# A bidirectional RWKV-7 step: the values' products move next to the first corner product, and the backward values come by DMA

## The chip, the cores and the metric

One core of a Trainium2 chip runs the whole kernel. The metric is the device time of one execution in microseconds; three executions of the kernel before took 2247.28, 2251.11 and 2251.58 us, so the median is 2251.11 us.

The core has five engines that work side by side, each through its own instruction queue in order: TensorE (PE, matmuls and transposes), VectorE (DVE), ScalarE (ACT), GpSimd (POOL) and SyncE (SP), which here issues nearly all DMAs. An instruction waits on semaphores for what other engines and DMAs have to finish, and all that stands behind it in its queue waits too.

## The reference

One layer of a hybrid model runs on 128 context tokens and 256 latent tokens, 384 in all, with 2048 channels in 32 heads of 64. One large input projection feeds an RWKV-7 branch (A) and a gated short convolution (B); both are projected, merged and projected again.

The part that matters is the scan of branch A. It runs once per direction `d`, with time reversed for `d = 1`:

```python
def step(S, inp):
    r_t, w_t, k_t, v_t, a_t, b_t = inp
    sa = jnp.einsum('dbhij,dbhj->dbhi', S, a_t)
    S = S * w_t[..., None, :] + sa[..., :, None] * b_t[..., None, :] + v_t[..., :, None] * k_t[..., None, :]
    y = jnp.einsum('dbhij,dbhj->dbhi', S, r_t)
    return S, y
```

`sa` is what a step removes from the state: it depends on the state, and so on all earlier values `v`. The values are the same in both directions, only their order in time differs.

## The kernel before, in words

**The stream.** All large products (input projection, output projections) are one long stream of matmuls on TensorE. Weights come as fp32 in halves of 1 MB (`wload`, L96, two `raw` buffers), are split by ACT and DVE into a high and a low fp32r part (`split`, L85, casts on L88, subtractions on L89, three buffers `whi` and `wlo`), and are used by three matmuls (L81 to L83). Three such matmuls are one unit, `ds_.go(n)` emits `n` units, and a quarter of a weight pair (one `whi` buffer) serves eight units, 24 matmuls.

**The blocks.** Sixteen blocks `b` of 128 channels (two heads) go through the scan, one after the other. A block's work is a set of generators: `prep_a` and `prep_k` (decays, keys), `prep_b` (chunk products and the inversion), `prep_c` (operands of the scan), `scan`, `norm`, `finish`. A generator says with `yield n` that `n` units of the stream stand between its pieces, and `drive` (L936) emits them. So the stream fills the time in which the scan waits for other engines.

**Chunks.** A direction has 384 tokens in 6 chunks of 64 tokens, so a block has 12 chunks, index `f` (0 to 5 forward, 6 to 11 backward). Within a chunk the steps become a triangular system. `A[:, 0, f, :]` holds its matrices: partitions 0 to 63 the part between removals, which must be inverted, and partitions 64 to 127 (`C:P`) the part that takes values to removals. `sav[:, f, :]` is the matching right side: partitions 64 to 127 hold the values with time on the partitions, partitions 0 to 63 the removals.

**The inversion.** Each triangular matrix is cut in 32 x 32 corners. `prep_b` writes them by DMA to DRAM (`ui`, L715) and reads them back as `U` with one corner per partition (L721). DVE eliminates column by column in 30 pairs of steps (L726, L728), and DMAs bring the inverses back into `A` (L739) and into `x11` (L740). `corner` in `scan` completes the inverse by two products of corners, `pH` and `pX` (L853).

**`prep_c` before the change.** It loads the initial states, then turns the values of both directions: three 128 x 128 transposes on TensorE (L760) of `v`, then three of `vr`, which ACT copies in reversed order from `v` (L757), and four ACT copies out of PSUM into `sav[C:P]` (L762). It turns `bk` (L769), computes the values' part of the removals by 24 products of 64 x 64 (`pav`, L775; each shows as two records) and copies them with four ACT copies into `sav[0:C]` (L779). POOL then clears `A[C:P, 0]` (L782), so that later products with all of `A[:, 0]` add no value twice.

**`scan` before the change.** It starts with `pH`, whose four copies into `x11` go to ACT and DVE in turn (L859). Then the latent chain is started (`chain(1)`: `po` L815, added to `sav` by DVE on L816), the bonus and `pX` follow, and both chains run: `pq` (L832) multiplies `A[:, 0, f]` with `sav[:, f]`, `pu` (L839) updates the states.

**What sets the order.** TensorE's order is written out by hand (`manual_schedule`, L73). The other queues, SP's among them, are ordered by a planner from dependencies, priorities and its own estimates; `scan` has a higher priority. `tc.issue_after(x)` keeps instructions behind `x` on its engine. Before `scan`, L972 to L974 fill the units since `prep_c` up to `WINDOW` = 80 (96 in the first and last block). PSUM tiles of the scans rotate through five banks (`bank`, L595).

Of the kernel before, what the change touches and what calls it, by code (L numbers as in the profile page):

```python
# [9 lines left out]
F32 = mybir.dt.float32  # L10
# [5 lines left out]
P = 128  # L16
D = 2048
KC = 16
T = 384
TC_ = 128  # L20
NB = 16
C = 64
NCH = 6
# [33 lines left out]
def hybrid_step(ctx, tc, cst, x_prompt, x_sample, state_f, state_b, c, c_ctx, ada_w, ada_b, norm_g,  # L57
                w_in, mu_prev, mu_next, w0, w2, a0, a2, k_k, k_a, r_k, lnx_g, lnx_b, conv_w,
                w_out_a, w_out_b, w_o, final_g, y_prompt, y_sample, ns_f, ns_b):
    nc = tc.nc  # L60
    V, S, G, TE = nc.vector, nc.scalar, nc.gpsimd, nc.tensor
# [8 lines left out]
    dp = ctx.enter_context(tc.tile_pool(name="dp", bufs=1, space=bass.MemoryType.DRAM))  # L70
# [5 lines left out]
    ident = cs[:, C_ID:C_ID + P]  # L76
# [176 lines left out]
    def pcol(i, n=1):  # L253
        return par[:, i:i + n]
# [151 lines left out]
    r_, k_, v_, ga_ = {}, {}, {}, {}  # L406
    box = {}

    def tmp(nm):
        return box["sp"].tile([P, T], F32, tag="t", name=nm, bufs=8)  # L410
# [141 lines left out]
    for i in range(3):  # L552
        t = tmp(f"lst_{i}")
# [4 lines left out]
    for m in range(4):  # L558
# [6 lines left out]
        t = tmp(f"lin_{m}")  # L565
# [3 lines left out]
        src = t[0:96, ::-1] if m % 2 else t[0:96, :]  # L569
# [23 lines left out]
    hss = [slice(0, C), slice(C, P)]  # L593

    def bank(nm):  # L595
        return ps1.tile([P, 4, P], F32, tag="A", name=nm, bufs=5)
# [4 lines left out]
    def flat(a):  # L601
        return a.rearrange("p n t -> p (n t)")
# [4 lines left out]
    def hl_parts(t, hi, nm):  # L607
        lo = sp.tile([P, T], F32R, tag="t", name=f"lo_{nm}", bufs=8)
        S.copy(hi[:], t[:])
        V.tensor_tensor(lo[:], t[:], hi[:].bitcast(F32), ALU.subtract)  # L610
        return hi, lo
# [129 lines left out]

    def prep_c(b, o):

        r, v, A = r_[b], v_[b], o["A"]
        for d in range(2):
            for h in range(2):
                nc.sync.dma_start(s_in[d][hss[h], hss[h]], ctx_st[d][0, 0, 2 * b + h])

        sav = sp.tile([P, 2 * NCH, P], F32, tag="sav", name=f"sav_{b}")
        bt = sp.tile([P, 2 * NCH, P], F32, tag="bt", name=f"bt_{b}")  # L750
        o["sav"], o["bkt"] = sav, bt
        for d in range(2):
            if d == 0:
                src = v
            else:
                src = tmp(f"vr_{b}")
                S.copy(src[:], v[:, ::-1])  # L757
            pv = bank(f"pv_{b}_{d}")
            for q in range(3):
                TE.transpose(pv[:, q, :], src[:, q * P:(q + 1) * P], ident)  # L760
            for e in range(2):
                S.copy(sav[C:P, NCH * d + e:NCH * d + NCH:2, :], pv[C * e:C * e + C, 0:3, :])  # L762
            yield 1
        for d in range(2):

            for n0, n1 in (((0, 4), (4, 5)), ((0, 3), (4, 6)))[d]:
                pb = bank(f"pb_{b}_{d}_{n0}")
                for n in range(n0, n1):
                    TE.transpose(pb[:, n - n0, :], o["bk"][d][:, n, :], ident)  # L769
                S.copy(bt[:, NCH * d + n0:NCH * d + n1, :], pb[:, 0:n1 - n0, :])  # L770
                yield 1
        pvs = [bank(f"pav_{b}_{d}") for d in range(2)]
        for f in range(2 * NCH):
            for h in range(2):
                TE.matmul(flat(pvs[f // NCH][hss[h]])[:, C * (f % NCH):C * (f % NCH) + C], A[C:P, 0, f, hss[h]],  # L775
                          sav[C:P, f, hss[h]], start=True, stop=True)
        for d in range(2):
            for h in range(2):
                S.copy(sav[0:C, NCH * d:NCH * d + NCH, hss[h]],  # L779
                       flat(pvs[d][hss[h]])[:, 0:NCH * C].rearrange("p (n i) -> p n i", i=C))  # L780

        G.memset(A[C:P, 0, :, :], 0.0)  # L782
        yield 2
        ks = o["kd"]
        V.tensor_tensor(ks[0][:], ks[0][:], ks[1][:, ::-1], ALU.add)
        V.scalar_tensor_tensor(ks[0][:], ks[0][:], pcol(RK + b), r[:], ALU.mult, ALU.mult)
        o["bsum"] = hl_parts(ks[0], sp.tile([P, T], F32R, tag="t", name=f"bsh_{b}", bufs=8), f"bs_{b}")
        yield 1
        pt = bank(f"psi_{b}")
        for d in range(2):  # L790
            TE.transpose(pt[:, d, :], s_in[d][:], ident)
        V.tensor_copy(st[1][:], pt[:, 0:2, :])
        yield 1

    def scan(b, o):
        A, x11, sav, bt = o["A"], o["x11"], o["sav"], o["bkt"]
# [51 lines left out]
        def corner(nm, lhs, rhs):  # L848
            pz = bank(f"{nm}_{b}")
            for f in range(2 * NCH):  # L850
                for h in range(2):
                    g = 32 * (2 * (f % 2) + h)
                    TE.matmul(flat(pz[g:g + 32])[:, 32 * (f // 2):32 * (f // 2) + 32], lhs(f, h), rhs(f, h),  # L853
                              start=True, stop=True)
            return [flat(pz[32 * j:32 * j + 32])[:, 0:192].rearrange("p (n t) -> p n t", t=32) for j in range(4)]

        pz = corner("pH", lambda f, h: A[0:32, 0, f, C * h + 32:C * h + C], lambda f, h: x11[0:32, 2 * f + h, :])
        for j in range(4):
            (S.copy, V.tensor_copy)[j % 2](x11[32:64, j::4, :], pz[j])  # L859
        yield H0  # L860
        lat = chain(1)
        next(lat)
# [9 lines left out]
        pz = corner("pX", lambda f, h: x11[32:64, 2 * f + h, :], lambda f, h: A[32:64, 0, f, C * h + 32:C * h + C])  # L872
# [16 lines left out]
        for q in range(3):  # L889
            for h in range(2):  # L890
                for d in range(2):
                    for e in range(2):
                        f = 2 * q + e if d == 0 else NCH + 5 - 2 * q - e
                        TE.matmul(py[hss[e], q, hss[h]], A[:, 1, f, hss[h]], sav[:, f, hss[h]],
                                  start=d == 0, stop=d == 1)
# [40 lines left out]
    def drive(gen, prio=0, at=None, fn=None):  # L936
        n = i = 0
        while True:
            if i == at:
                fn()  # L940
            i += 1
            with tc.high_priority(offset=prio):
                u = next(gen, None)
            if u is None:
                return n
            ds_.go(u)
            n += u
# [6 lines left out]
    for b in range(NB):  # L954
# [10 lines left out]
        n = drive(prep_c(b, cur))  # L965
# [140 lines left out]
    for half in range(2):  # L1106
# [8 lines left out]
        for s in range(3):  # L1115
# [10 lines left out]
            if half == 1:  # L1126
                f = rsf[:, s, :]
# [37 lines left out]
```

## Time and profile before

| | |
|---|---|
| time, median of three runs | 2251.11 us |
| time of the profiled execution | 2248.96 us |
| its span, first to last instruction | 2247.2 us |
| TensorE busy | 2187.8 us, 97% |
| VectorE busy | 1522.3 us, 68% |
| ScalarE busy | 1060.1 us, 47% |
| GpSimd busy | 115.7 us, 5% |
| granted TensorE clock | 0.996 |
| moved by DMA | 339.96 MB, mean 151 GB/s |

A row of the timeline has start, duration, engine, line, operation, out<-in and a count; in brackets stands the idle time before it and what ended it. `d_...` are matmuls of the stream. An engine with a `q` (SPq) is a queue issuing a DMA, and the duration is that of the issue, not of the transfer. A row of a group has the busy time and the mean duration in ns after the bar. A row of the DMA view has the size in KB and the median time from issue to landing in us. Matmuls overlap: the time between two starts says how long one takes, a single duration does not.

### The profile page before, as it was taken

How to read it: one execution, taken by the hardware profiler on the slowest of the kernel's cores; microseconds unless marked ns; L12 is line 12 of the kernel's file. 1: busy time of each engine (PE TensorE's matmuls, PEld its weight loads, DVE VectorE, ACT ScalarE, POOL GpSimd, SP SyncE). 2: the span in 40 equal slices, each digit the busy share in tenths (PEclk: the TensorE clock that was granted, in tenths of full speed). 3: DMA queues.
4: the chain of work that ended last, by engine and by line, in shares of the span. 5: the costliest groups of instructions: out<-in, count | busy, mean ns of one | idle time of the engine just before them, and what ended most of it. 6: DMA issues, size and time to landing. Idle time of an engine off the chain costs nothing.

```text
span 2247.2 us, 40428 instructions
## 1 busy us (share of the span) xinstructions
PE 2187.8 (97%) x16084; PEld 2072.0 (92%) x16084; DVE 1522.3 (68%) x3096; ACT 1060.1 (47%) x1864; POOL 115.7 (5%) x115
## 2 busy tenths in 40 slices
PE   5999999999999999999999999999999999999998
PEld 3688999999999999999999999999999999998988
DVE  3248567787777778777878787777777775444354
ACT  4245445454545455454545454546455543333333
POOL 2000010101010100000010101010100000000000
PEclk9999999999999999999999999999999999999999
DMA  9963544444444444353444444444445465886633
GB/s 337 346 205 116 147 129 132 111 127 116 110 126 118 115 117 130 112 133 102 124 108 130 114 111 131 111 115 136 127 119 143 137 184 154 289 293 230 220 131 113
DMA packets 429644, 339.96 MB, mean 151 GB/s; under 512 B 84800, under 2 KB 411024, under 8 KB 428560
## 3 DMA queue, kind: packets, MB, share of 16 engines
q1 hardware_dynamic: 427968, 335.62, 50.9%
q8 instruction: 127, 2.08, 0.4%
q10 hardware_dynamic: 432, 1.57, 0.2%
q14 instruction: 61, 0.50, 0.1%
q0 software_dynamic: 1056, 0.19, 0.1%
HBM read 307.37 MB, written 29.36 MB: 150 GB/s over the span
## 4 chain that ended last, share of the span: by engine, by line
PE 81%; DVE 7%; DMA 7%; ACT 3%; issue 1%; SPq 1%; POOLq 0%; POOL 0%; ACTq 0%; DVEq 0%
PE d_rk L81 4%; PE d_rk L83 4%; PE d_rk L82 4%; PE d_gv L81 4%; PE d_gv L82 4%; PE d_gv L83 4%; DMA raw_adah<-in_ada_w_dram 3%; PE pA L705 2%; PE d_oa L81 2%; PE d_oa L83 2%; PE d_oa L82 2%; PE d_bc L81 2%; PE d_bg L81 2%; DMA lraw<-in_w_dram 2%; PE d_bc L82 2%; PE d_bc L83 2%
## 5 line engine op out<-in xcount | busy, mean ns | idle before, releaser
L81 PE MATMUL d_rk<-h_hi,whi_rk 128*128 128x384 f32 x480 | 164.3, 342 | 0.6 <-ACT lst L554 0.6
L726 DVE TENSOR_TENSOR ut<-U 48x30 f32<-48x30 f32 (+14 forms) x480 | 154.5, 322 | 15.3 <-DMA U<-ui 3.0
L728 DVE TENSOR_TENSOR U<-U,ut 48x30 f32<-48x30 f32 (+14 forms) x480 | 154.3, 321 | 11.2
L81 PE MATMUL d_gv<-h_hi,whi_gv 128*128 128x384 f32 x480 | 161.4, 336 | 0.0
L83 PE MATMUL d_gv<-h_hi,wlo_gv 128*128 128x384 f32 x480 | 161.2, 336 | 0.0
L82 PE MATMUL d_gv<-h_lo,whi_gv 128*128 128x384 f32 x480 | 161.1, 336 | 0.0
L83 PE MATMUL d_rk<-h_hi,wlo_rk 128*128 128x384 f32 x480 | 160.6, 335 | 0.0
L82 PE MATMUL d_rk<-h_lo,whi_rk 128*128 128x384 f32 x480 | 160.6, 334 | 0.0
L88 ACT CAST whi_gv<-raw_gv 128x1024 fp32r<-128x1024 f32 (+1 forms) x64 | 63.9, 999 | 139.3 <-PE d_rk L82 90.9
L89 DVE TENSOR_TENSOR wlo_rk<-raw_rk,whi_rk 128x1024 fp32r<-128x1024 f32 x60 | 72.9, 1218 | 44.6 <-ACT whi_rk L88 38.9
L88 ACT CAST whi_rk<-raw_rk 128x1024 fp32r<-128x1024 f32 x60 | 63.0, 1053 | 80.0 <-PE d_bc L82 16.4
L81 PE MATMUL d_bc<-h_hi,whi_bc 128*128 128x384 f32 x256 | 92.5, 361 | 0.0
L81 PE MATMUL d_gb<-h_hi,whi_gb 128*128 128x384 f32 x256 | 92.5, 361 | 0.0
L81 PE MATMUL d_bg<-h_hi,whi_bg 128*128 128x384 f32 x256 | 92.4, 361 | 0.0
L81 PE MATMUL d_bx<-h_hi,whi_bx 128*128 128x384 f32 x256 | 92.4, 361 | 0.0
L81 PE MATMUL d_ma<-h_hi,whi_ma 128*128 128x384 f32 x256 | 92.0, 359 | 0.0
L81 PEld LDWEIGHTS d_rk<-h_hi,whi_rk 128*128 128x128 f32 x480 | 90.1, 188 | 1.8 <-ACT lst L554 0.9
L922 POOL TENSOR_TENSOR rs<-var,nhalf 128x6 f32<-128x6 f32 x16 | 21.2, 1325 | 1362.3 <-DVE var L920 1362.3
L81 PEld LDWEIGHTS d_gv<-h_hi,whi_gv 128*128 128x128 f32 x480 | 90.7, 189 | 0.2
L82 PEld LDWEIGHTS d_gv<-h_lo,whi_gv 128*128 128x128 f32 x480 | 90.7, 189 | 0.0
L83 PEld LDWEIGHTS d_gv<-h_hi,wlo_gv 128*128 128x128 f32 x480 | 90.7, 189 | 0.0
L81 PE MATMUL d_mb<-h_hi,whi_mb 128*128 128x384 f32 x256 | 90.6, 354 | 0.0
(320 smaller groups left out, 6655.4 us busy)
## 6 DMA issues: line engine op xcount, KB each, us to landing
raw_adah<-in_ada_w_dram SPq DMA_DIRECT2D x64, 512.0 KB, 8.7
raw_rk<-in_w_in_dram SPq DMA_DIRECT2D x60, 512.0 KB, 5.3
raw_gv<-in_w_in_dram SPq DMA_DIRECT2D x60, 512.0 KB, 5.0
raw_ma<-in_w_in_dram SPq DMA_DIRECT2D x16, 1024.0 KB, 5.6
raw_mb<-in_w_in_dram SPq DMA_DIRECT2D x16, 1024.0 KB, 5.5
raw_bc<-in_w_in_dram SPq DMA_DIRECT2D x16, 1024.0 KB, 5.5
raw_bx<-in_w_in_dram SPq DMA_DIRECT2D x16, 1024.0 KB, 5.3
raw_bg<-in_w_in_dram SPq DMA_DIRECT2D x16, 1024.0 KB, 5.6
```

The costliest lines, as they stand in the source:

```text
L81: TE.matmul(out, wh, xh, start=start, stop=False)
L82: TE.matmul(out, wh, xl, start=False, stop=False)
L83: TE.matmul(out, wl, xh, start=False, stop=stop)
L88: S.copy(hi[0:rows], src)
L89: V.tensor_tensor(lo[0:rows], src, hi[0:rows].bitcast(F32), ALU.subtract)
L705: TE.matmul(pas[h, n // 4 * 4][:, n % 4, :], bk[hss[h], n, :], pr[hss[h], n, :], start=True, stop=True)
L726: V.tensor_tensor(tv, U[:, 0:s, s:s + 1].broadcast_to([48, s, w]), U[:, s:s + 1, s + 1:].broadcast_to([48, s, w]), ALU.mult)
L728: V.tensor_tensor(U[:, 0:s, s + 1:], U[:, 0:s, s + 1:], tv, ALU.add)
L922: G.tensor_tensor(rs[:], var[:], nhalf[:], ALU.pow)
```

## The change

- The values are turned once. The copy to `vr`, its three transposes and its two copies out of PSUM go, and with them one `yield 1`.
- The backward values are made by three DMAs on SP, one after the other: the forward values from `sav` to a DRAM tile `vt` (tokens by channels), `vt` with reversed rows to a DRAM tile `vr`, and `vr` to the backward chunks of `sav`. Each moves 192 KB; the middle one goes in pieces of 64 channels, 256 B.
- The 24 `pav` products move from `prep_c` to the start of `scan`, right ahead of `pH`. Their four ACT copies stand behind the last ACT copy into `x11`, and the clearing of `A[C:P, 0]` follows. `prep_c` loses one `yield 2`.

```diff
     def prep_c(b, o):
 
-        r, v, A = r_[b], v_[b], o["A"]
+        r, v = r_[b], v_[b]
...
-        for d in range(2):
-            if d == 0:
-                src = v
-            else:
-                src = tmp(f"vr_{b}")
-                S.copy(src[:], v[:, ::-1])
-            pv = bank(f"pv_{b}_{d}")
-            for q in range(3):
-                TE.transpose(pv[:, q, :], src[:, q * P:(q + 1) * P], ident)
-            for e in range(2):
-                S.copy(sav[C:P, NCH * d + e:NCH * d + NCH:2, :], pv[C * e:C * e + C, 0:3, :])
-            yield 1
+        pv = bank(f"pv_{b}")
+        for q in range(3):
+            TE.transpose(pv[:, q, :], v[:, q * P:(q + 1) * P], ident)
+        for e in range(2):
+            S.copy(sav[C:P, e:NCH:2, :], pv[C * e:C * e + C, 0:3, :])
+
+        vt = dp.tile([T, P], F32, tag="vt", name=f"vt_{b}", bufs=2)
+        vr = dp.tile([T, P], F32, tag="vr", name=f"vr_{b}", bufs=2)
+        nc.sync.dma_start(vt[:].rearrange("(n s) c -> s n c", s=C), sav[C:P, 0:NCH, :])
+        nc.sync.dma_start(vr[:].rearrange("t (h c) -> h t c", h=2), vt[::-1, :].rearrange("t (h c) -> h t c", h=2))
+        nc.sync.dma_start(sav[C:P, NCH:2 * NCH, :], vr[:].rearrange("(n s) c -> s n c", s=C))
+        yield 1
...
-        pvs = [bank(f"pav_{b}_{d}") for d in range(2)]
-        for f in range(2 * NCH):
-            for h in range(2):
-                TE.matmul(flat(pvs[f // NCH][hss[h]])[:, C * (f % NCH):C * (f % NCH) + C], A[C:P, 0, f, hss[h]],
-                          sav[C:P, f, hss[h]], start=True, stop=True)
-        for d in range(2):
-            for h in range(2):
-                S.copy(sav[0:C, NCH * d:NCH * d + NCH, hss[h]],
-                       flat(pvs[d][hss[h]])[:, 0:NCH * C].rearrange("p (n i) -> p n i", i=C))
-
-        G.memset(A[C:P, 0, :, :], 0.0)
-        yield 2
...
+        pvs = [bank(f"pav_{b}_{d}") for d in range(2)]
+        for f in range(2 * NCH):
+            for h in range(2):
+                TE.matmul(flat(pvs[f // NCH][hss[h]])[:, C * (f % NCH):C * (f % NCH) + C], A[C:P, 0, f, hss[h]],
+                          sav[C:P, f, hss[h]], start=True, stop=True)
+        xs = None
         pz = corner("pH", lambda f, h: A[0:32, 0, f, C * h + 32:C * h + C], lambda f, h: x11[0:32, 2 * f + h, :])
         for j in range(4):
-            (S.copy, V.tensor_copy)[j % 2](x11[32:64, j::4, :], pz[j])
+            x = (S.copy, V.tensor_copy)[j % 2](x11[32:64, j::4, :], pz[j])
+            xs = x if j % 2 == 0 else xs
+        with tc.issue_after(xs.ins):
+            for d in range(2):
+                for h in range(2):
+                    S.copy(sav[0:C, NCH * d:NCH * d + NCH, hss[h]],
+                           flat(pvs[d][hss[h]])[:, 0:NCH * C].rearrange("p (n i) -> p n i", i=C))
+
+        G.memset(A[C:P, 0, :, :], 0.0)
         yield H0
```

## The prediction

> **What bounds the kernel now.** I read the page first: span, engines, the chain that ended last.
>
> ```profile
> span 2247.2 us, 40428 instructions
> ...
> PE 2187.8 (97%) x16084; PEld 2072.0 (92%) x16084; DVE 1522.3 (68%) x3096; ACT 1060.1 (47%) x1864; POOL 115.7 (5%) x115
> ...
> q1 hardware_dynamic: 427968, 335.62, 50.9%
> ...
> PE 81%; DVE 7%; DMA 7%; ACT 3%; issue 1%; SPq 1%; POOLq 0%; POOL 0%; ACTq 0%; DVEq 0%
> ```
>
> TensorE is busy 97% of the span and holds 81% of the chain. Next came TensorE's own waits between 200 and 1860 us, where the sixteen scans lie (releaser: total us, times, longest); its two largest rows are
>
> ```profile
> PE pu L839 <- ACT sav L834: 4.8, 11, 0.6
> PE pv L760 <- DVE A L711: 1.7, 1, 1.7
> ```
>
> In 1660 us TensorE waits for almost nothing. So what leaves its order shortens the kernel one for one, and only a new wait of TensorE can lengthen it. The other engines matter through such waits alone.
>
> **The change, part by part.** *The second turning leaves.* TensorE's timeline around it (start, duration, engine, line, count), in the block whose scan starts at 1004 us:
>
> ```profile
> 956.19 0.34 PE L83 MATMUL d_bc<-h_hi,wlo_bc 128*128 128x384 f32 x1
> 956.36 0.49 PE L760 MATMUL pv<-cs,vr 128*128 128x128 f32 x3
> 956.61 0.42 PE L81 MATMUL d_bc<-h_hi,whi_bc 128*128 128x384 f32 x1
> 956.87 0.34 PE L82 MATMUL d_bc<-h_lo,whi_bc 128*128 128x384 f32 x1
> ```
>
> and around the values' products, which move:
>
> ```profile
> 960.25 0.34 PE L83 MATMUL d_rk<-h_hi,wlo_rk 128*128 128x384 f32 x1
> 960.52 1.61 PE L775 MATMUL pav<-sav,A 64*64 64x64 f32 x48
> 962.06 0.45 PE L81 MATMUL d_rk<-h_hi,whi_rk 128*128 128x384 f32 x1
> 962.35 0.34 PE L82 MATMUL d_rk<-h_lo,whi_rk 128*128 128x384 f32 x1
> 962.52 0.34 PE L83 MATMUL d_rk<-h_hi,wlo_rk 128*128 128x384 f32 x1
> 962.70 0.33 PE L81 MATMUL d_rk<-h_hi,whi_rk 128*128 128x384 f32 x1
> ```
>
> Starts, not durations, are to be read, since matmuls overlap. Two plain steps of the stream take 0.35 us (962.35 to 962.70). With the three transposes of `vr` between, two steps take 956.87 - 956.19 = 0.68, so the turning costs 0.33 us a block, and 16 x 0.33 = **5.3 us** go. Its ACT work (one reversing copy, two copies out of PSUM) goes too, and is worth nothing: ACT is at 47% and no such wait stands above.
>
> *The burst.* The products alone cost 962.35 - 960.25 - 0.35 = 1.75 us. How much of it is entering and leaving? The first corner product, before which they are put, and the mean of one matmul in each group (after the bar: busy us, mean ns):
>
> ```profile
> 1003.81 0.34 PE L639 MATMUL pn<-lo_sq,bones_r 128*128 128x384 f32 x1
> 1004.08 0.62 PE L853 MATMUL pH<-x,A 32*32 32x32 f32 x48
> 1004.63 0.45 PE L81 MATMUL d_bx<-h_hi,whi_bx 128*128 128x384 f32 x1
> 1004.91 0.34 PE L82 MATMUL d_bx<-h_lo,whi_bx 128*128 128x384 f32 x1
> ```
> ```profile
> L775 PE MATMUL pav<-sav,A 64*64 64x64 f32 x768 | 25.8, 220 | 0.0
> L853 PE MATMUL pH<-x,A 32*32 32x32 f32 x768 | 9.9, 194 | 0.0
> ```
>
> The corner costs 1004.91 - 1003.81 - 0.35 = 0.75. From its first start to its last the `pav` group runs 1.61 - 0.22 = 1.39, the corner 0.62 - 0.19 = 0.43. What is left, 0.36 and 0.32, is a burst's fixed price, and one of the two can be saved. Upper bound 0.34 a block (passing from 64x64 to 32x32 tiles is free), lower bound 0 (it costs as much as leaving the stream and coming back). The rows show two parts of that price: the way in (0.27 to the first small matmul instead of 0.17, so 0.10) and the way back (962.06 to 962.35, 0.29 instead of 0.17, so 0.12). A change of tile size is still a way in, while one way back surely goes, with some of the emptying before it; I take 0.20, nearer to the way back. That is **3.2 us** over 16 blocks, bounds 0 and 5.4. The Trainium skill speaks against more (TensorEngine Tiling (Array Packing), Tiling Modes, Key Properties): changing the tiling mode, not just the tile, drains the TensorE. Taken strictly, the saving would be the lower bound, and the whole change worth the 5.3 us alone; no row here has two tile sizes next to each other.
>
> *Three units fewer in the preparation.* A unit is three matmuls of the stream. `prep_c` asks for 10 now and 7 then, but a block is filled up to 80 (`WINDOW`), so the three come back before the scan: moved, not saved.
>
> *What moves onto the scan's start.* The four `sav` copies, now ACT's after the second `x` copy, the POOL memset, and who needs them:
>
> ```profile
> L779 ACT COPY sav<-pav 64x384 f32<-64x384 f32 x64 | 30.4, 476 | 3.1 <-PE pav L775 2.3
> ```
> ```profile
> 1005.47 0.31 ACT L859 COPY x<-pH 32x192 f32<-32x192 f32 x1 [0.42 <-DVE x L859]
> 1007.30 1.05 ACT L88 CAST whi_bg<-raw_bg 128x1024 fp32r<-128x1024 f32 x1 [1.52 <-PE d_bx L82]
> ```
> ```profile
> 962.25 1.38 POOL L782 MEMSET A<- 64x1536 f32 x1 [8.24 <-DVE ut L726]
> ```
> ```profile
> 1011.50 0.61 PE L832 MATMUL pq<-sav,A 128*128 128x128 f32 x4
> ```
>
> The copies take 4 x 0.476 = 1.9 us: 1005.8 to 1007.7, of which 1.5 fill ACT's idle time ahead of the cast, which starts 0.4 later. DVE's sum into `sav` (L816) waits behind them with all that is queued after it on DVE, the next `wlo` first, which itself waits for that cast. The memset would end near 1005.6. TensorE asks for `sav` and `A` at 1011.5. Cover 3.8 us or more, so 0; without cover a late copy would cost TensorE its lateness once a block.
>
> *The three transfers.* No row has a DRAM-to-DRAM one. The nearest (KB, median us to landing), the copies after which the chain can start, and SP's queue there:
>
> ```profile
> uo<-U SPq DMA_DIRECT2D x16, 192.0 KB, 2.5
> U<-ui SPq DMA_DIRECT2D x16, 192.0 KB, 5.1
> ```
> ```profile
> 956.04 0.96 ACT L762 COPY sav<-pv 64x384 f32<-64x384 f32 x2 [1.01 <-PE pv L760]
> ```
> ```profile
> 956.88 0.45 SPq L721 DMA_DIRECT2D U<-ui  x1
> ...
> 968.62 1.02 SPq L104 DMA_DIRECT2D raw_gv<-in_w_in_dram  x2
> ```
>
> Each of the three waits on SP for the one before it. Lower bound 3 x 2.5 = 7.5 us. The middle one moves 768 pieces of 256 B. A packet takes 0.509 x 16 x 2247.2 us / 427968 = 43 ns on its engine on average; spread over 16 engines that is 2 us, over two engines 16 us. Upper bound 5.1 + (16.4 + 2.5) + 5.1 = 29. From 957.0 on, the values stand in `sav` by 965 to 986, and the burst wants them at 1002.3 (1004.08 - 1.75): no wait at either end. I take 9 us. What counts is SP, which issues nothing while it waits. The `U` load at 956.88 is ready as the copies end and, by this order, goes first. The next weights are issued at 968.62 and cast at 978.57:
>
> ```profile
> raw_gv<-in_w_in_dram SPq DMA_DIRECT2D x2, 512.0 KB, 4.7
> ```
> ```profile
> 978.57 1.06 ACT L88 CAST whi_gv<-raw_gv 128x1024 fp32r<-128x1024 f32 x1 [0.95 <-PE d_rk L82]
> ```
> ```profile
> 981.02 1.21 DVE L89 TENSOR_TENSOR wlo_gv<-raw_gv,whi_gv 128x1024 fp32r<-128x1024 f32 x1
> ```
>
> They land near 974, 4.5 us before the cast, which waits for TensorE to free a buffer, not for the DMA. With three buffers two quarters are then still ahead of it, 2 x 24 matmuls of 0.175 us, 8.4 us, of which cast and subtraction take 3.7 (978.57 to 982.23): another 4.7 us of cover. So these weights may come 9.2 us late, and a hold of SP of some 9 us, which is over before 968.6, costs 0. The three issues themselves are 0.4 to 1.0 us each on SP, as the rows of `U` and `x` show.
>
> *The corner's input.* TensorE now comes to `pH` 0.53 us earlier, and `x11` has to be there. Its last transfer in two blocks (issue; median us to landing in that window) and the other block's `pH`:
>
> ```profile
> 1000.19 0.91 SPq L740 DMA_DIRECT2D x<-uo  x1
> ```
> ```profile
> x<-uo SPq DMA_DIRECT2D x1, 48.0 KB, 3.5
> ```
> ```profile
> 1527.86 0.47 SPq L740 DMA_DIRECT2D x<-uo  x1
> ```
> ```profile
> x<-uo SPq DMA_DIRECT2D x1, 48.0 KB, 2.1
> ```
> ```profile
> 1532.96 0.62 PE L853 MATMUL pH<-x,A 32*32 32x32 f32 x48
> ```
>
> It lands at 1003.7, 0.4 us before `pH`; in the other block at 1530.0, 3.0 us before. These two stand for thirteen middle blocks: ten of the first kind (landing 0.3 to 1.2 ahead), three of the second (2.5 to 3.0). Blocks 0, 1 and 15 have more. If nothing else shifts, the earlier arrival waits 0.1 to 0.3 in four or five blocks, **0.5 us** in all. The cover is thin: any delay of the chain from `ui` to `x11` is paid at once in ten blocks.
>
> **Sum.** 5.3 + 3.2 - 0.5 = 8.0. The profiled execution took 2248.96 us (span 2247.2 and 1.8 around it): 2241.0. The median of the runs, 2251.11, is 2.15 higher, which gives 2243.1 on that footing. I say **2242**.
>
> **Rivals.** (a) *The wait moves to the corner: no change.* If the planner puts the first values' transfer ahead of the `U` load, that load goes out after the copies (957.0) and one issue, 0.5 us late, and has 192 KB more before it on the same DMA engines, 0.7 us at the 293 GB/s that the 16 engines reach while they are busy (335.62 MB in 50.9% of 2247.2 us). With 0.8 us of delay the ten blocks wait about 0.7 each: 8.0 - 7 = 1, 2248 to 2250. For it: both are ready within 0.2 us of each other. Against it: `U` is the older work.
>
> (b) *The chain of transfers holds what TensorE needs: slower.* Place: SP, ahead of the `U` load, with the second values' transfer there too. `U` then waits for the copies, an issue, a landing of 2.5 and another issue: 957.0 + 0.4 + 2.5 + 0.6 = 960.5, 3.6 late. Ten blocks then lose 3.5 each, three about 1: 38 us, less 8.5, is 2278. From 0.4 us of delay on, a block like the one at 1004 has lost its gain, so that the sign turns between (a) and (b). Against it: the second transfer is ready 3 us after `U` is.
>
> (c) *The middle transfer is slow: slower.* On two engines it holds SP, from 957.0, for the first transfer (0.4 + 2.5), its own issue (0.6) and 18.9, and the last issue (0.4), to 979.8. The weights of 968.62 come 11.2 us late, 2.0 more than their cover, and 13 blocks lose 26: 2267. The gain is gone once that wait is 0.6 a block, that is from a hold of about 21 us. For it, the Trainium skill (DMA: Bandwidth & Descriptors, Why a DMA increments its semaphore by 16 and not by 1) says the engines used are the largest number up to 16 that divides the slowest dimension of both patterns, and this transfer's slowest dimension is 2. Against it: pieces of 256 B are a third of the 784 B of the mean packet, and should take less than 43 ns.
>
> (d) *More than I sum:* tile sizes change for free and nothing waits: 5.3 + 5.4, 2238 to 2240.
>
> **How the numbers follow.** Forecast 0.47, (a) 0.23, (b) 0.09, (c) 0.08, (d) 0.08; 0.05 for an order of SP or DVE of which I see nothing, even either way. 0.2% (4.5 us) is about what a measurement of this kernel can tell from no change: faster is below 2246.6. The forecast's own range is 2237 to 2246.5 (sum 5 to 11, on either footing); nearly all of it, of (d) and a little of (a) is faster: 0.56. Same is most of (a) and the forecast's upper edge: 0.25. Slower is (b), (c) and the rest: 0.19. The range runs from 2235 to 2257, which leaves out (b), (c) and little below.
>
> **What would show it.** Right: 48 fewer `pv` matmuls; `pav` and `pH` side by side, from the last stream start to the second after them 2.3 + 0.35 us (2.5 without a saving, 2.16 with a full one); no wait of TensorE for a DMA at `pav` or `pH` over some tenths; `sav` copies over 3 us ahead of `pq`. Wrong: TensorE waiting at L853 for `x` in ten blocks (a, b), or casts waiting for `raw` after the values' transfers (c); and where that middle transfer needs over 10 us, my 9 for the chain is wrong even if it stays hidden.

## The result, and the profile after

The changed kernel takes 2545.59 us (median of five runs, 2544.41 to 2546.56) against 2251.11: a ratio of 1.1315, 95% interval 1.1299 to 1.133. Forecast were 2242 us. The profiled execution took 2546.3 us.

The page of the changed kernel: span, engines, the clock in 40 slices, the chain that ended last.

```profile
span 2544.4 us, 40349 instructions
...
PE 2219.1 (87%) x16036; PEld 2096.5 (82%) x16036; DVE 1530.4 (60%) x3096; ACT 1036.7 (41%) x1816; POOL 121.4 (5%) x115
...
PEclk9998989998989898989898989898989899999999
...
PE 56%; DVE 22%; DMA 11%; ACT 5%; issue 3%; SPq 2%; DVEq 0%; POOLq 0%; POOL 0%; ACTq 0%
```

TensorE held 81% of the chain and holds 56% now; DVE and DMA have taken the rest. TensorE has 48 instructions fewer and is busy 31.3 us longer, and its clock dips once a block. Its waits say where the rest went (releaser: total us, times, longest):

```profile
PE d_gv L81 <- ACT whi_gv L88: 248.6, 14, 18.5
...
PE d_ma L81 <- ACT whi_ma L88: 12.8, 1, 12.8
...
PE d_gv L83 <- DVE wlo_gv L89: 3.5, 14, 0.3
```

248.6 + 12.8 + 3.5 = 264.9 us of waiting for freshly cast weights, and 31.3 us more of busy time: 296.2 of the 297.3 us by which the two profiled executions differ. In each of fourteen blocks TensorE stands still once, some 18 us long. ACT's timeline in one of them says what the cast waits for:

```profile
1012.70 1.99 ACT L88 CAST whi_gv<-raw_gv 128x1024 fp32r<-128x1024 f32 x2 [11.11 <-DMA raw_gv<-in_w_in_dram]
```

and SP's timeline in the same block why those weights are late:

```profile
967.29 0.88 SPq L721 DMA_DIRECT2D U<-ui  x1
968.26 0.63 SPq L760 DMA_DIRECT2D vt<-sav  x1
968.94 0.61 SPq L104 DMA_DIRECT2D raw_gv<-in_w_in_dram  x1
...
972.66 0.62 SPq L761 DMA_DIRECT2D vr<-vt  x1
999.66 0.32 SPq L733 DMA_DIRECT2D uo<-U  x1
1001.62 0.30 SPq L734 DMA_DIRECT2D uo<-UT  x1
1002.03 0.63 SPq L762 DMA_DIRECT2D sav<-vr  x1
...
1005.87 0.47 SPq L740 DMA_DIRECT2D x<-uo  x1
1006.38 1.10 SPq L104 DMA_DIRECT2D raw_gv<-in_w_in_dram  x2
```

SP issues nothing from 973.3 to 999.66. It does not wait for the middle transfer there: the next instruction in its queue is the store of the inverse, which waits for DVE's elimination, and the second half of the weights, issued at 968.62 in the kernel before (23 us ahead of that store, the row below), now stands behind it.

```profile
991.53 0.34 SPq L733 DMA_DIRECT2D uo<-U  x1
```

Counted from the load of `U` these weights are issued 968.62 - 956.88 = 11.7 us later in the kernel before, and 1006.38 - 967.29 = 39.1 here: 27.4 us late, of which the cover of 9.2 that the prediction worked out takes its part. What is left is 18.2, and a stall takes 248.6 / 14 = 17.8. SP's own waits for the elimination, after and then before:

```profile
SPq L733 <- DVE U L728: 357.1, 16, 26.5
```
```profile
SPq L733 <- DVE U L728: 84.8, 16, 6.8
```

The stretches of that block (from, to and length in us; the busy time of PE, PEld, DVE, ACT and POOL in this order, with the instructions of each in parentheses; then granted TensorE clock, DMA share, GB/s):

```profile
980.00:985.00 5.00, 5.00 (x31) 5.00 (x30) 4.76 (x11) 1.09 (x2) 0.00 (x0) 1.00 0.01 2
...
995.00:1000.00 5.00, 0.33 (x2) 0.01 (x1) 4.15 (x17) 0.33 (x1) 0.00 (x0) 0.86 0.00 0
1000.00:1005.00 5.00, 0.00 (x0) 0.00 (x0) 0.00 (x0) 1.59 (x1) 0.00 (x0) 0.50 0.61 137
1005.00:1010.00 5.00, 0.00 (x0) 0.00 (x0) 0.00 (x0) 0.00 (x0) 0.00 (x0) 0.50 0.70 159
1010.00:1015.00 5.00, 1.01 (x2) 0.50 (x2) 1.22 (x2) 1.99 (x2) 0.00 (x0) 0.50 1.06 310
1015.00:1020.00 5.00, 4.94 (x18) 4.94 (x19) 2.36 (x3) 1.04 (x1) 0.00 (x0) 0.59 0.51 157
```

From 980 on the DMA engines move next to nothing (2 GB/s): the middle transfer was over some 7.5 us after its issue. TensorE stops shortly after 995, and when the weights come it starts again at half its clock (0.50, then 0.59). That is what makes it busy longer with fewer instructions: the matmuls of `d_gv` alone, which stand behind these stalls, are busy 526.6 us in place of 483.7.

What the change was to save is in the trace all the same. The burst of the block whose scan starts at 1034 us:

```profile
1033.63 0.34 PE L639 MATMUL pn<-lo_sq,bones_r 128*128 128x384 f32 x1
1033.90 1.61 PE L849 MATMUL pav<-sav,A 64*64 64x64 f32 x48
1035.45 0.62 PE L841 MATMUL pH<-x,A 32*32 32x32 f32 x48
1036.00 0.44 PE L81 MATMUL d_bg<-h_hi,whi_bg 128*128 128x384 f32 x1
1036.27 0.33 PE L82 MATMUL d_bg<-h_lo,whi_bg 128*128 128x384 f32 x1
```

1036.27 - 1033.63 - 0.35 = 2.29 us, where the two groups apart cost 1.75 + 0.75 = 2.50: 0.21 saved.

### The profile page after: what moved, and what is told of

It reads as the page before. It is cut to its first block, busy times and chain, and to the rows that moved or that the text cites. A ratio compares the mean times of both kernels' runs of the same rounds, so it can differ in the third digit from the quotient of the medians.

```text
span 2544.4 us, 40349 instructions
## 1 busy us (share of the span) xinstructions
PE 2219.1 (87%) x16036; PEld 2096.5 (82%) x16036; DVE 1530.4 (60%) x3096; ACT 1036.7 (41%) x1816; POOL 121.4 (5%) x115
## 4 chain that ended last, share of the span: by engine, by line
PE 56%; DVE 22%; DMA 11%; ACT 5%; issue 3%; SPq 2%; DVEq 0%; POOLq 0%; POOL 0%; ACTq 0%
DVE U L728 5%; DVE ut L726 5%; DMA raw_gv<-in_w_in_dram 3%; DMA raw_adah<-in_ada_w_dram 3%; PE d_gv L83 2%; PE d_gv L81 2%; PE d_gv L82 2%; DVE wlo_gv L89 2%; PE d_bx L81 2%; PE d_oa L81 2%; PE pA L705 2%; PE d_bx L83 2%; PE d_bx L82 2%; PE d_oa L83 2%; PE d_oa L82 2%
## 5 line engine op out<-in xcount | busy, mean ns | idle before, releaser
L81 PE MATMUL d_gv<-h_hi,whi_gv 128*128 128x384 f32 x480 | 177.2, 369 | 248.6 <-ACT whi_gv L88 248.6
L81 PEld LDWEIGHTS d_gv<-h_hi,whi_gv 128*128 128x128 f32 x480 | 101.1, 211 | 253.3 <-ACT whi_gv L88 253.1
L89 DVE TENSOR_TENSOR wlo_gv<-raw_gv,whi_gv 128x1024 fp32r<-128x1024 f32 (+1 forms) x64 | 72.5, 1150 | 204.4 <-ACT whi_gv L88 204.4
L83 PE MATMUL d_gv<-h_hi,wlo_gv 128*128 128x384 f32 x480 | 175.2, 365 | 3.5 <-DVE wlo_gv L89 3.5
L82 PE MATMUL d_gv<-h_lo,whi_gv 128*128 128x384 f32 x480 | 174.2, 363 | 0.0
L83 PEld LDWEIGHTS d_gv<-h_hi,wlo_gv 128*128 128x128 f32 x480 | 100.1, 208 | 10.6 <-DVE wlo_gv L89 10.6
L81 PE MATMUL d_ma<-h_hi,whi_ma 128*128 128x384 f32 x256 | 92.5, 361 | 12.8 <-ACT whi_ma L88 12.8
L82 PEld LDWEIGHTS d_gv<-h_lo,whi_gv 128*128 128x128 f32 x480 | 100.9, 210 | 0.0
L81 PE MATMUL d_ob<-ybh,whi_ob 128*128 128x384 f32 x256 | 88.5, 346 | 3.9 <-ACT whi_ob L88 2.7
```

Of the source, the lines that this page charges most:

```text
L81: TE.matmul(out, wh, xh, start=start, stop=False)
L82: TE.matmul(out, wh, xl, start=False, stop=False)
L83: TE.matmul(out, wl, xh, start=False, stop=stop)
L89: V.tensor_tensor(lo[0:rows], src, hi[0:rows].bitcast(F32), ALU.subtract)
```

## The experiments

Each was timed next to the kernel before on its own chip; those medians lie between 2249.2 and 2250.2 us. `gv` are the weights of the gate and the values.

### SP's order alone, no part of the change

The second half of each pair of `gv` weights is told to issue behind the last load of `x11`; the rest of the kernel before stays.

```diff
+        late = nm.startswith("gv") and nm.endswith("_1") and "xd" in box
+        with tc.issue_after(box["xd"]) if late else ExitStack():
             ...the loads of raw...
+        box["xd"] = xd.ins        # the last load of x11
```

> The kernel before with one edit: each block's second half of the gv weights may be issued on SP only after that block's last x11 load. No values' transfer, no burst, the same arithmetic; SP's order of weights and inverse DMAs becomes that of the changed kernel. Theory A (the loss is SP's planned order: weights queued behind the inverse's DMAs, which wait for DVE's elimination): TensorE waits some 17 to 18 us a block at whi_gv and the time is near 2545, +280 to +310 us. Theory B (the transfers themselves take the DMA engines or SP from the weights): no transfer is there, so under +30 us. Theory C (the burst and its copies): no change.

2510.8 us, ratio 1.1164 (1.1143 to 1.1184).

```profile
PE d_gv L81 <- ACT whi_gv L88: 217.8, 14, 16.7
```
```profile
PE 2232.6 (89%) x16084; PEld 2105.9 (84%) x16084; DVE 1530.2 (61%) x3096; ACT 1059.3 (42%) x1864; POOL 115.5 (5%) x115
```

The order alone costs 261 of the 294 us (2545.59 - 2251.11), less than the 280 to 310 expected, with the same waits at the same place, and TensorE is 44.8 us longer busy than in the kernel before with the same instructions: the half clock again. The spans of the two profiled executions differ by 34.2 us: the changed kernel waits 30.8 more at the same place and 12.8 at `whi_ma`, and is busy 13.5 less. That TensorE gets there earlier (the products no longer stand ahead of that place) and that `sav<-vr` is one more issue ahead of the weights could make the longer waits; this was not tried apart.

### The reversal: without it, and in sixteen column groups

Two kernels, each with one edit to the changed one. The first does not reverse the rows, so the backward scan works on forward values. The second reverses in pieces of 8 channels (32 B).

```diff
-  dma_start(vr.rearrange("t (h c) -> h t c", h=2), vt[::-1, :].rearrange("t (h c) -> h t c", h=2))
+  dma_start(vr.rearrange("t (h c) -> h t c", h=2), vt[:, :].rearrange("t (h c) -> h t c", h=2))     # first
+  dma_start(vr.rearrange("t (h c) -> h t c", h=16), vt[::-1, :].rearrange("t (h c) -> h t c", h=16)) # second
```

> The changed kernel, but the middle transfer copies vt to vr in the same pieces without reversing the rows, so the backward values keep forward order (that part of the result is left out). If the reversal costs, the time falls to about 2243. If the two halves of channels as slowest dimension cost, it stays at 2545 within 5 us, with the same order on SP and the 256 B pieces again through in some 7 us.

> The changed kernel, reversed by 16 groups of 8 channels instead of 2 of 64: the slowest dimension is 16, the pieces are 32 B and 6144 of them. The planner's order on SP is then that of the kernel before. Theory A: the stalls at whi_gv are gone and the sum of the prediction holds, -8 us, 2241 to 2244. Theory B: 384 pieces an engine as before, so a transfer of 4 to 7 us on all 16 engines that delays the U load and the weights; a gain of at most 3 us, or a loss. Theory C: still slower than before.

First: 2543.38 us, in one execution. Second: 2252.98 us, ratio 1.0018 (1.0009 to 1.0027). SP's order between the load of `U` and that of `x11` in a middle block (states and `A` left out; a `gv` is what is left of the loads of one half):

```
before                 U      gv     gv      gb gb  uo uo  bc  x x
changed, not reversed  U  vt  gv vr                 uo uo  sav  x x  gv gb gb
sixteen groups         U  vt  gv vr  gv sav  gb gb  uo uo  bc  x x
```

So it is not the reversal: with a slowest dimension of 2 and pieces of 256 B the planner puts the weights behind the inverse, with 16 and 32 B it does not. That it goes by its own price for the transfer is inferred from that order, not seen. The transfer itself hardly differs: with sixteen groups it lands 7.0 us after issue, with two after some 7.5.

```profile
vr<-vt SPq DMA_DIRECT2D x16, 192.0 KB, 7.0
```

This is most of the loss, but not all: the eight microseconds that TensorE saves do not show with sixteen groups either.

### The three transfers on GpSimd's queue

As in the change, with `nc.gpsimd.dma_start` for the three, and two column groups.

> The change with its three transfers issued by GpSimd's own queue instead of SyncE's; the two column groups, and so the two engines that carry the middle transfer, stay. Theory A (SyncE's order alone made the loss): the weights keep their place ahead of the inverse's stores, no wait of whi_gv over 1 us, 2250 to 2256, as with sixteen groups. Rival B (two engines busy for 7 us with 256-byte packets delay the weights' packets behind them): waits at whi_gv of 3 us or more in most of 14 blocks, 2290 or more. The unit count is that of the change, so pl waits of some 5 us in all stay.

2290.55 us, ratio 1.0186 (1.0172 to 1.02): the number of the rival, but not by its mechanism. In the scans no wait for `whi_gv` is left; the largest wait is

```profile
PE pq L820 <- issue: 15.5, 9, 1.7
```

So with the 256 B pieces TensorE waits for no cast of `gv`, though the loads of `gv` land in 6.7 us, where they took 5.0 before. What makes `pq` late is in ACT's rows: the wait of the small casts for the next block's `pl` in sum, and one of them.

```profile
ACT lwh L88 <- DMA lraw<-in_w_dram: 55.5, 13, 6.4
```
```profile
1022.82 0.41 ACT L88 CAST lwh<-lraw 96x256 fp32r<-96x256 f32 x1 [5.50 <-DMA lraw<-in_w_dram]
1023.25 0.31 ACT L854 COPY x<-pH 32x192 f32<-32x192 f32 x1
```

In that block `pH` starts at 1019.59. ACT's first copy of it stands behind a cast whose weights have not landed, and with it the `sav` copies and all up to `pq` at 1029.54. With sixteen groups the same row has 4.8 us in 3 waits. This is a second queue that the planner ordered anew; it is read from the trace, no run took that order apart.

### The burst alone, and the break behind it

Four kernels, to find where the eight microseconds stay. First the burst moved alone, without the transfers (the second turning stays); then the same, and the whole change in sixteen groups, with the `yield 2` that the change drops left in `prep_c` (and, with sixteen groups, two units in place of one behind the turning); and the kernel before with nothing but that `yield 2` taken out. The last one's edit:

```diff
         G.memset(A[C:P, 0, :, :], 0.0)
-        yield 2
```

> The kernel before with the values' products moved next to the first corner product, and the second turning kept: no transfer. In the changed kernel pn, pav and pH cost 2.635 us together, before 1.750 + 1.102 apart, so 0.217 a block is saved: -3.5 us, 2246 to 2248. Theory C: slower than before.

> The kernel before with only the values' products moved next to the first corner product (second turning kept, no transfers), and the break of two stream units that stood behind them left in the preparation, at its old place. Theory U (units): the run without that break lost because the next block's decay and mixing products (pl) then come to TensorE too early after their casts (5.0 us of waits of pl for lwl in 8 places); with the break kept these waits fall under 1.5 us and the 0.217 us a block that the burst saves show: 2246 to 2249. Rival (the copies and the memset on the scan's start, or the planner's new order around the corner's input, cost what the burst saves): the same time as without the break, 2253 to 2257.

> The whole change, with the reversal cut into 16 column groups in place of 2, and the break of two stream units kept in the preparation (and the break behind the one turning that is left made two units instead of one, so that the number of units is as before). Theory U: waits of pl for lwl under 1.5 us, and the 0.33 + 0.217 us a block show: 2250 - 8.8 + 0.5 = 2241 to 2244. Rival (what is put on the scan's start, or the corner's input, which TensorE now reaches 0.55 us a block earlier and before it has landed): 2249 to 2253, with waits at pH for x of 0.3 us or more in ten blocks.

> The kernel before with one edit: the break of two stream units behind the values' products and the memset is left out; every product, copy and transfer stays. Theory U: pl then waits for lwl in some 8 places, 3 to 5 us in all, and the kernel takes 2252 to 2257. Rival: the break is made up before the scan, as my sum had it (moved, not saved), and the time stays within 2 us of the kernel before.

2256.03 (ratio 1.0034, 1.0022 to 1.0047), 2256.24 (1.0027, 1.0017 to 1.0038), 2256.06 (1.0032, 1.002 to 1.0045), and 2250.67 us (1.0003, 0.9994 to 1.0012). The theory of the break falls: without it the kernel before is as it was, with it the moved burst still loses. The burst's move itself costs, though it saves 0.21 us a block on TensorE. What it costs shows in every second block, at the products `pl` for the next block's decays. First the burst with the break kept, then the kernel before (TensorE and ACT, the same block):

```profile
1106.54 0.44 PE L81 MATMUL pl<-l_hi,lwh 96*128 96x384 f32 x1 [0.74 <-ACT lwh L88]
...
1107.80 0.44 PE L83 MATMUL pl<-l_hi,lwl 96*128 96x384 f32 x1 [0.65 <-DVE lwl L89]
```
```profile
1101.32 2.11 ACT L732 COPY UT<-U 48x1024 f32<-48x1024 f32 x1 [2.34 <-DVE U L728]
...
1106.09 0.40 ACT L88 CAST lwh<-lraw 96x256 fp32r<-96x256 f32 x1
```
```profile
1099.46 2.14 ACT L732 COPY UT<-U 48x1024 f32<-48x1024 f32 x1 [1.20 <-DVE U L728]
...
1104.63 0.40 ACT L88 CAST lwh<-lraw 96x256 fp32r<-96x256 f32 x1
```

```profile
1101.41 0.34 PE L81 MATMUL pl<-l_hi,lwh 96*128 96x384 f32 x1
```
```profile
1102.38 0.34 PE L81 MATMUL pl<-l_hi,lwh 96*128 96x384 f32 x1
```

The cast for the third `pl` stands on ACT behind the copy `UT`, and that waits for the elimination. The last two rows are the first `pl`, with the burst moved and before: it came 2.92 us behind the start of that copy (1102.38 - 1099.46), and comes 0.09 behind it now. Of these 2.83 us 1.75 are the products, which TensorE does between the load of `U` and `pl` in the kernel before and behind `pl` when they are moved. Of the other 1.1 a longer elimination makes 1.0. The subtractions of L89 alone on DVE in that elimination, kernel before and burst moved (from, to, length, busy and count):

```profile
1068.55:1099.18 30.63, 8.48 (x7) 1.00 0.41 120
```
```profile
1069.40:1101.04 31.64, 9.67 (x8) 1.00 0.40 118
```

All of DVE in the first of them, the third busy time of the row:

```profile
1068.55:1099.18 30.63, 30.63 (x179) 30.60 (x178) 29.25 (x77) 12.31 (x19) 1.24 (x1) 1.00 0.41 120
```

DVE is full there, so what the stream puts into its queue lengthens the inverse. TensorE is further in its stream all through the elimination, and the subtraction that came just behind its end now falls into it: eight instead of seven. The new theory: these blocks are bound by the inverse's chain through DVE, ACT and SP, and what TensorE saves is waited away at `pl` and at `pH`.

### The chain cut short: the elimination's last six steps left out

In the kernel before and in the one with sixteen groups (the inverse, and so the result, is another).

```diff
-        for s in range(1, 31):
+        for s in range(1, 25):
```

> The kernel before with the last six of the elimination's thirty steps left out (the inverse, and with it the result, is another; some 3.0 us of DVE work a block, just ahead of the copy UT). Theory V (TensorE sets the pace before; the inverse's chain through DVE keeps up by 0.3 to 1.2 us in every second block): nothing to gain, 2246 to 2250. Rival (the chain bounds the kernel before as well): 2244 or less.

> The change with sixteen column groups (SyncE's order as before), and the last six of the elimination's thirty steps left out (the inverse, and with it the result, is another). Theory V: moved behind pl, the values' products bring TensorE to pl and pH 1.75 and 0.55 us earlier against the inverse's chain, and DVE then takes one more subtraction of 1.2 us into the elimination of every second block; the chain ends late there, and the 0.55 us a block that TensorE saves are waited away at pl and at x. With 3 us of the elimination gone these waits go, and the saving shows: 2240 to 2244. Rival W (the copies and the memset on the scan's start or the transfers cost what was saved): 2250 to 2254, as with the whole elimination.

2245.95 us (ratio 0.9984, 0.9975 to 0.9993) and 2237.5 us (0.9946, 0.9934 to 0.9959). With the chain out of the way the change is worth 2245.95 - 2237.5 = 8.5 us. The kernel before gains 4 us, a little more than expected. That the chain already held it back somewhat is not shown: the profile of the kernel before has only 0.4 us of waits at `pl` and none at `pH`.

### Less work for DVE: two subtractions on GpSimd

Two of the subtractions in each elimination go to GpSimd, with sixteen groups and in the kernel before.

```diff
-        V.tensor_tensor(lo[0:rows], src, hi[0:rows].bitcast(F32), ALU.subtract)
+        E.tensor_tensor(lo[0:rows], src, hi[0:rows].bitcast(F32), ALU.subtract)   # E = G for gv's second quarters
```

> The change with sixteen column groups, whole, and two of the eight weight subtractions that fall into each elimination (the second quarter of each gv half) put on GpSimd in place of DVE. Theory V: DVE has 2.4 us less in the elimination, which ends by as much earlier, pl and pH wait no more, and the time is 2240 to 2246, below the kernel before. GpSimd's part takes some 2.0 us by the rate of its product of 768 columns (1.53 us); if that comes late, TensorE waits at d_gv for POOL's wlo_gv instead, in up to 30 places, and the time is 2252 or more. Rival W: no change from 2250 to 2254 with no such waits.

> The kernel before with the same two subtractions on GpSimd, as the control of the run with sixteen groups. Theory V: TensorE sets the pace, so 2247 to 2251, or more if GpSimd's subtractions come late. Rival (DVE bounds the kernel before): 2244 or less.

2291.68 (1.0188, 1.0174 to 1.0202) and 2268.88 us (1.0087, 1.0073 to 1.01), both worse. With sixteen groups TensorE waits most for DVE's products of the gate. The group on GpSimd in the kernel before:

```profile
L89 POOL TENSOR_TENSOR wlo_gv<-raw_gv,whi_gv 128x1024 fp32r<-128x1024 f32 x28 | 107.3, 3834 | 260.7 <-ACT whi_gv L88 205.4 <-DVE ut L727 43.3 <-DVE U L729 12.0
```

3.83 us instead of the 2.0 estimated, and 2.53 with sixteen groups: this says nothing on the chain, only that GpSimd is no place for them.

### The chain made shorter, with the result unchanged

`UT`'s first 24 columns are copied before the elimination ends (the ones on the diagonal are added first, no step reads them); or the casts for `pl` get two buffers (the scratch of the elimination is trimmed and the norm's three small tiles share one, to make room); or both.

```diff
+            if s == 23:
+                S.copy(UT[:, 0:24, :], U[:, :, 0:24].rearrange("p a b -> p b a"))
...
-        S.copy(UT[:], U[:].rearrange("p a b -> p b a"))
+        S.copy(UT[:, 24:32, :], U[:, :, 24:32].rearrange("p a b -> p b a"))
```

> The kernel before with the copy UT in two parts: its first 24 columns, which no step after the 23rd changes, before the elimination's end, the last 8 at the end (the diagonal's ones are added at the start, where no step reads them). The inverse's chain gets some 1.5 us shorter (2.14 us of copy become about 0.6 behind the elimination), the result stays. Theory V (TensorE sets the pace before, with 0.3 to 1.2 us to spare in every second block): 2246 to 2250. Rival (DVE and ACT bound it already): 2243 or less.

> The whole change with sixteen column groups, and the copy UT in two parts as in the other kernel. Theory V: in every second block the chain was 1.2 us late; 1.5 us less of it lets most of the 8 us show, 2240 to 2246, with the waits at pl and pH under 3 us together. Rival (only the DVE part counts; the copy on ACT and what follows are hidden): 2250 to 2254.

> The whole change with sixteen column groups, and two buffers for the casts of pl (lwh and lwl; to make room the scratch of the elimination is cut to the 240 columns it uses, and the norm's three small tiles share one), so that they no longer wait behind the copy UT. Theory V: the waits at pl (6 us) vanish, but TensorE then comes to pH before x has landed, and waits there instead: 2249 to 2253, pH waits of 5 us or more. Rival (the single cast buffer alone took the gain): 2240 to 2245.

> The whole change with sixteen column groups, the copy UT in two parts and two buffers for the casts of pl. Theory V: no more than a few us below the kernel with the copy in two parts alone, 2238 to 2245. Rival (neither matters): 2250 to 2254.

2247.71 us for the kernel before with the copy in two parts (ratio 0.9999, 0.999 to 1.0007), and with sixteen groups 2247.72 (0.9991, 0.9983 to 1.0), 2248.37 (0.9995, 0.9986 to 1.0004) and 2250.74 us (1.0, 0.9991 to 1.0009). The waits at `pl` are gone in all three but for one of 0.6 us, and one wait has taken their place, here with the copy in two parts:

```profile
PE pH L843 <- DMA x<-uo: 5.5, 8, 1.4
```

The next link of the chain, the landing of `x11`. Only part of the gain shows: about as much as expected with the two buffers, less than expected with the copy and with both. The runs of each of these kernels spread over 5 to 8 us, so the three are not told apart.

These waits cost more than their length. In that kernel the products `pH` stop half-way, and this is the clock (the last number but two) ahead of the second half and behind its start:

```profile
477.47 0.55 PE L843 MATMUL pH<-x,A 32*32 32x32 f32 x24 [1.42 <-DMA x<-uo]
```
```profile
474.00:477.50 3.50, 2.08 (x78) 1.79 (x77) 0.89 (x2) 0.89 (x2) 1.37 (x1) 1.00 0.58 86
477.50:480.90 3.40, 3.40 (x33) 3.34 (x34) 0.71 (x2) 2.33 (x6) 0.00 (x0) 0.50 0.92 308
```

For 3.4 us TensorE works at half its clock, which costs another 1.7 us. The same follows the waits in three other blocks, 6.8 us in all beside the 5.5 of waiting; after a wait of 0.46 at 901.6 it does not.

### And `x11` ahead of `A`

On SP the two loads of `x11` go ahead of the four loads of `A`, with the copy in two parts, without and with the change in sixteen groups.

```diff
         for d in range(2):
+            x = nc.sync.dma_start(x11[0:32, 12 * d:12 * d + 12, :], uo[1, d, 0].rearrange("i s t -> s i t"))
+        with tc.issue_after(x.ins):
+            for d in range(2):
                 for e in range(2):
                     nc.sync.dma_start(blocks(A, d, e), uo[0, d, e].rearrange("i s t -> s i t"))
-            nc.sync.dma_start(x11[0:32, 12 * d:12 * d + 12, :], uo[1, d, 0].rearrange("i s t -> s i t"))
```

> The kernel before with the copy UT in two parts and, on SyncE, the two loads of x11 ahead of the four loads of A (which are told to go behind them). Theory V: TensorE sets the pace, 2245 to 2249, no wait at pH.

> The whole change with sixteen column groups, the copy UT in two parts, and x11's two loads ahead of A's four. x11 lands some 2 us earlier (two pairs of loads of A stood before its last load, 1.12 and 0.98 us on SyncE). Theory V: the waits at pH go (under 1 us), and the time is 2238 to 2242, 6 to 9 us under the same kernel without the change. Rival (something else takes the gain): 2246 to 2250 as with A first.

2246.41 us (0.9984, 0.9975 to 0.9992) and 2237.82 us (0.9951, 0.9937 to 0.9965). The second is below every other kernel here with its result unchanged, by 8.6 us of its twin without the change and 12 of the kernel before. Its profile: span and engines, SP behind the elimination, and the longest of TensorE's waits in the scans.

```profile
span 2233.1 us, 40332 instructions
...
PE 2176.8 (97%) x16036; PEld 2065.9 (93%) x16036; DVE 1521.9 (68%) x3096; ACT 1038.1 (46%) x1832; POOL 120.4 (5%) x115
```
```profile
1098.86 0.91 SPq L740 DMA_DIRECT2D x<-uo  x2
1099.87 3.28 SPq L744 DMA_DIRECT2D A<-uo  x4
```
```profile
PE po L807 <- DVE st L836: 2.5, 7, 0.8
```

At `pH` no wait is left and at `pl` one of 0.5 us, and TensorE is busy 11.0 us less than in the kernel before. Between 200 and 1900 us its clock does not dip any more. Against the same kernel with `A` first the span is 12.4 us shorter, where 5.5 of waits and 6.8 of half clock have gone.

## Why the prediction was wrong, point by point

- **The failed step** is the sentence on the transfers: "a hold of SP of some 9 us, which is over before 968.6, costs 0". It put the three transfers into SP's queue and left all else in it where it stood. The transfers took longer than 9 us: 4.4 from the first issue to the second, 7.5 for the middle one, 3.4 for the last to land. But it was not that which cost: the planner moved the weights of 968.62 behind the inverse's stores, and SP then waited for DVE until 999.66. The cover of 9.2 us worked out for those weights was right in kind, but they came 27.4 us late: a stall of 18 a block, as that cover gives it. The order alone, without the change, costs 261 us.
- **Rival (c)** named the place (SP, casts waiting for `raw` after the values' transfers) and took the wrong mechanism: the transfer took 7.5 us, not 18.9, and the price was 294 us, not 26. The DMA view of the changed kernel from 975 to 980 us, while that transfer runs (packets, MB, share of 16 engines):

```profile
q1 hardware_dynamic: 659, 0.17, 14.8%
```

  14.8% of sixteen are 2.4 engines. The Trainium skill's rule (DMA: Bandwidth & Descriptors, Why a DMA increments its semaphore by 16 and not by 1) has this shape on two; the trace is near that but cannot count engines, since the share adds up packet times that overlap (1.06 in the row from 1010 us above). What was wrong is the packet: 0.148 x 16 x 5 us / 659 = 18 ns, where the mean of 43 ns was taken.
- **The second failed step** is the term of 0.5 us for the corner's input. With SP's order restored the whole change is 3.5 us slower than the kernel before, where 8.0 faster was the sum: that term is some 12 us (8.5 + 3.5), and 9.6 of them stand in that kernel's profile as waits at `pl` and `pH`. Counted was that TensorE comes to `pH` 0.53 us earlier; left out was that it comes to all that lies between the products' old and new place 1.75 us earlier, the next block's `pl` among it, and that DVE then takes one more subtraction into the elimination. "Any delay of the chain from `ui` to `x11` is paid at once in ten blocks" was written there, and the delay was not looked for.
- **The turning and the burst** were sized right: 0.21 measured for the burst's 0.20, and together 8.5 us (short elimination) and 8.6 us (`x11` ahead) for the sum's 8.5 before its deduction. That these agree to a tenth is luck: the runs of these kernels spread over 3 to 7 us. Of a burst's price of 0.32 to 0.36 us, 0.21 was saved where two tile sizes stand next to each other, so the strict reading, by which nothing would have been saved, did not hold.
- **"Moved, not saved"** for the units of the preparation holds: taking the break out changes nothing (1.0003). The `sav` copies and the memset on the scan's start cost nothing that shows: in the last kernel `pq` does not appear among the larger waits.
- (a) and (b) did not come: the first values' transfer went out behind the load of `U`, as assumed. (d) did not come either.
- That TensorE sets the pace alone in the kernel before was nearly right: with six steps of the elimination left out it gains 4 us of 2250.

## What to carry to other kernels

Where a planner orders a queue, an added DMA is not one more entry in the old order: compare the orders of all queues before trusting any cover, and above all what now stands behind an instruction that waits long. Work taken from an engine's path is worth its time only where no other chain is due at the same moment; work that is moved from one side of such a chain to the other shifts everything between by its full length, not by what the move saves. To see what a change is worth, loosen the second chain in both kernels and compare those.

## What the hardware showed beside that

- In the stall shown the granted clock fell from 1.00 to 0.50 at 998.6 us, 3.3 us after TensorE's last matmul had ended (995.3). The first matmul behind the stall started at 1013.80, and the clock stayed at 0.50 until 1019, 5.2 us. In the kernel with nothing but SP's order changed such stalls left TensorE 44.8 us longer busy. The Trainium skill (TensorE: Matmul & The Clock Gate, What's actually happening) has the half rate after an idle window of about 3.4 us and the full rate after as much sustained work. The trace agrees on the fall; the way back took longer here.
- A wait need not be that long. Inside the burst of 64 x 64 and 32 x 32 products, a wait of 1.42 us, and in another block two of 0.16 and 0.22, was followed by 3.4 us at a clock of 0.50; without waits the same burst left the clock at 1.00. What decides it is not shown.
- A subtraction of 128 x 1024 fp32 took GpSimd 3.83 us in the kernel before and 2.53 with sixteen groups, where 2.0 was estimated from the rate of its 128 x 768 product (1.53 us). The Trainium skill (SBUF — State Buffer, Who interferes with whom) has DVE's instructions with two SBUF inputs contend with GpSimd's reads; the rows fit, but no run here took that apart.
